# Attention stages: the low parts of the weights move to GpSimd, and the softmax's bias addition and row maximum become one VectorE instruction

## The chip, the cores and the metric

The kernel runs on one core of a Trainium2 chip. The metric is the device time of one execution in microseconds (us). Engines are named as in the profile: PE is TensorE (PEld its weight loads), DVE is VectorE, ACT is ScalarE, POOL is GpSimd, SP is SyncE, which issues the DMAs.

## The reference

The kernel computes a decoder trunk of two layers on 512 tokens of width 1024, with 16 heads of 64. Both layers add attention, a SwiGLU feed-forward part and a gated per-layer embedding to the residual `h`. Layer 0 attends by stick-breaking, layer 1 by a softmax with forget gates:

```python
# layer 0, mixer A
z = einsum('bhqd,bhkd->bhqk', qb, k) * scale
log_one_minus = where(strict, -softplus(z), 0.0)
later = cumsum(log_one_minus, axis=3, reverse=True) - log_one_minus
w = where(strict, exp(log_sigmoid(z) + later), 0.0)
out = einsum('bhqk,bhkd->bhqd', w, v)
# layer 1, mixer B
logits = einsum('bhqd,bhkd->bhqk', qb, k) * scale + fb[..., :, None] - f_cum[:, :, None, :]
logits = where(causal, logits, -inf)
out = einsum('bhqk,bhkd->bhqd', softmax(logits, axis=-1), v)
# both layers, afterwards
h = h + out @ w_o
h = h + (silu(g) * u) @ w_d          # g, u from rms(h) @ w_gu
h = h + sigmoid(rms(h) @ w_gate) * (p[i] @ w_proj)
```

The term `fb[..., :, None]` is the same for a whole row of the logits, so a softmax over the row does not change when it is left out.

## The kernel before

Every dense product is made of three matmuls, because each operand is split into a rounded high part and a remainder: `wh·xh`, `wh·xl` and `wl·xh` (L246 to L248; L389 to L391 where tokens are the rows). The weights arrive in 216 units of 128x1024. For each unit `load_unit` issues the DMA into `raw`, multiplies `raw` by a gain on POOL for 24 units of layer 1 (L144), casts it to `wh` on ACT (L147), and subtracts, `wl = raw - wh`, on DVE through `minus` (L125). `raw`, `wh` and `wl` have three buffers each, and units are loaded two ahead of their use.

An attention stage goes over 16 heads. `front(hd)` makes the scores of a head in three tiles `z` in PSUM: 512 wide, 384 wide, and one of 256 and 128 together; so there are four segments to a head. In layer 0 ACT forms two sigmoids `e` and `w` of a tile, DVE runs a scan over `e` for each segment (L638) and multiplies `w` by it (L641). In layer 1 DVE adds to `z` a per-row number `ngt` and a per-column row `gb` (L645), takes the maximum of each row (L651) and negates it (L653); ACT makes the exponential with that as bias and with a row sum (L655), DVE the reciprocal, and ACT the scaling. `back(hd)` turns the weights of the head with PE transposes (`pt`, L692) in three groups of four, four and two blocks, splits each group into a high part on ACT (`w3h`, `w2h`, `w1h`, L693) and a remainder on DVE (`w3l`, `w2l`, `w1l`, through `minus`, L125), and multiplies both by the values into `po` (L700, L701). Between these steps a `Filler` emits matmuls of later projections, so that PE has work while a head's chain runs on DVE and ACT.

`forget()` stands before the heads of layer 1. It makes the cumulated gate `gex` with a scan (L481) and a subtraction (L482), writes it to DRAM (`gdram`), from where `front` reads a row per head into `gb`, and transposes it on PE into `ngt` (L490 to L492).

A framework scheduler decides in which order instructions stand in each engine's queue; each engine runs its queue in that order. The score tiles have two PSUM buffers in layer 0 and one in layer 1 (`ZB = (2, 1)`): in layer 1 PE can begin a tile only when DVE has read the one before. `LOW` says per layer which engine forms `wl` while an attention stage's `state["low"]` holds; the other stages use DVE.

Of the kernel before, what the change touches and what calls it, by code (L numbers as in the profile page):

```python
# [18 lines left out]
F32 = mybir.dt.float32  # L19
F32R = mybir.dt.float32r  # L20
AF = mybir.ActivationFunctionType
ALU = mybir.AluOpType
PSUM = bass.MemoryType.PSUM

P = 128
S = 512
# [14 lines left out]
C_KG, C_QG, C_BF = 56, 57, 58  # L41
# [44 lines left out]
def trunk(ctx, tc, xT, pT, small, wf, wall, out, dump=None):  # L86
    nc = tc.nc
# [9 lines left out]
    sm = const.tile([P, NG], F32, name="sm")  # L97
# [4 lines left out]
    ident = const.tile([P, P], F32, name="ident")  # L102
    make_identity(nc, ident)

    identb = const.tile([P, P], BF16, name="identb")
    nc.vector.tensor_copy(identb, ident)
    masks = []
    for i, op in enumerate((ALU.is_gt, ALU.is_ge)):
        mf = tp.tile([P, S], F32, name="mf", tag="ta")
        nc.gpsimd.memset(mf[:, :P], 0.0)  # L110
        nc.gpsimd.affine_select(out=mf[:, :P], in_=mf[:, :P], pattern=[[1, P]], compare_op=op,
                                fill=-1.0e30, base=0, channel_multiplier=-1)
        mb = const.tile([P, P], BF16, name=f"mask{i}")
        nc.vector.tensor_copy(mb, mf[:, :P])
        masks.append(mb)
    one = const.tile([P, 1], F32, name="one")
    nc.vector.memset(one, 1.0)
    gq8 = const.tile([P, 1], F32, name="gq8")
    nc.vector.tensor_scalar_mul(gq8, sm[:, C_QG:C_QG + 1], 0.125)

    def table(name):
        tc.keep_in_program_order(nc.scalar.preload_act_table_set(name))
# [14 lines left out]
    def load_unit(u):  # L137
        if u not in raws:
            fetch(u)
        raw = raws.pop(u)  # L140
        if u in gains:
            c0, nk = gains[u]
            r3 = raw.rearrange("p (k n) -> p k n", k=nk)
            nc.gpsimd.tensor_tensor(  # L144
                r3, r3, sm[:, c0:c0 + nk].unsqueeze(2).to_broadcast([P, nk, 1024 // nk]), ALU.mult)
        wh = wpool.tile([P, 1024], F32R, name=f"wh{u}", tag="wh")
        nc.scalar.copy(wh, raw)  # L147
        wl = wpool.tile([P, 1024], F32R, name=f"wl{u}", tag="wl")
        if state["low"] == "gpsimd":
            for c in range(0, 1024, 256):  # L150
                nc.gpsimd.tensor_tensor(wl[:, c:c + 256], raw[:, c:c + 256],
                                        wh[:, c:c + 256].bitcast(F32), ALU.subtract)
        else:
            minus(wl, raw, wh)
        units[u] = (wh, wl)
# [200 lines left out]
    def attention(layer, buf):  # L356
# [3 lines left out]
        with tc.tile_pool(name=f"pa{layer}", bufs=1, space=PSUM, reuse_waits="tile") as pa, \  # L360
# [62 lines left out]
            if stick:  # L423
# [4 lines left out]
                m, r = norm_sums(pz, "z")  # L428
# [30 lines left out]
            def forget():  # L459
# [19 lines left out]
                nc.vector.scalar_tensor_tensor(zf[:16], zf[:16], 0.0, ef[:16], ALU.min, ALU.subtract)  # L479
                gex = tp.tile([P, S], F32, name="gex", tag="ta")[:16]  # L480
                nc.vector.tensor_tensor_scan(gex, zf[:16], zf[:16], 0.0, ALU.add, ALU.bypass)  # L481
                nc.vector.tensor_tensor(gex, gex, zf[:16], ALU.subtract)  # L482
                if "gex" in dump:
                    nc.sync.dma_start(dump["gex"], gex)
                gdram = dpool.tile([16, S], F32, name="gdram")
                nc.sync.dma_start(gdram, gex)
                ngt = a1.tile([P, 4, 16], F32, name="ngt")
                gps = pz.tile([P, S], F32, name="gps", tag="n", bufs=1)
                for j in range(4):
                    nc.tensor.transpose(gps[:, j * 16:(j + 1) * 16], gex[:, j * P:(j + 1) * P],  # L490
                                        ident[:16, :16])
                nc.vector.tensor_scalar_mul(ngt, gps[:, :64].rearrange("p (j n) -> p j n", j=4), -1.0)  # L492
                return gdram, ngt

            dd = {}

# [119 lines left out]
            def front(hd):  # L616
# [6 lines left out]
                for ti, segs in enumerate(TILES):  # L623
# [5 lines left out]
                    z = z[:, :n]  # L629
# [11 lines left out]
                            nc.vector.tensor_tensor(w[:, c + 1:c + m], w[:, c + 1:c + m],  # L641
                                                    e[:, c:c + m - 1], ALU.mult)
                    else:
                        for j, c, m in segs:
                            nc.vector.scalar_tensor_tensor(  # L645
                                w[:, c:c + m], z[:, c:c + m], ngt[:, j, hd:hd + 1], gb[:, j * P:],
                                ALU.add, ALU.add)
                        mx = a2.tile([P, 4], F32, name="mx", tag="mx", bufs=4)
                        ns = len(segs)
                        for si, (j, c, m) in enumerate(segs):  # L650
                            nc.vector.tensor_reduce(mx[:, si:si + 1], w[:, c:c + m],  # L651
                                                    mybir.AxisListType.X, ALU.max)
                        nc.vector.tensor_scalar_mul(mx[:, :ns], mx[:, :ns], -1.0)  # L653
                        for si, (j, c, m) in enumerate(segs):
                            nc.scalar.activation(w[:, c:c + m], w[:, c:c + m], AF.Exp,  # L655
                                                 bias=mx[:, si:si + 1], accum_out=mx[:, 2 + si:3 + si])
                        nc.vector.reciprocal(mx[:, 2:2 + ns], mx[:, 2:2 + ns])
                        for si, (j, c, m) in enumerate(segs):
# [66 lines left out]
            if stick:  # L725
                run(raw_qk(0))
            else:
                def sums():
                    m, tok["r"] = norm_sums()

                    tok["em"] = a1.tile([P, 4], F32, name="em")
                    nc.vector.tensor_scalar_mul(tok["em"], m, EPS)

                run(group(0, sums))
                rb = norm_bounce(tok["r"])
                run(expand(0))
                gdram, ngt = forget()
            for e in attn_order(layer)[3 if stick else 2:]:
                i = int(e[1:])
                fill.add(e, (raw_qk(i) if i < RAW_PAIRS else qk(i)) if e[0] == "p" else expand(i) if e[0] == "e" else  # L740
# [59 lines left out]


AHEAD = 2
LOW = ("vector", "vector")
ZB = (2, 1)
TB = (2, 2)
WB = (6, 5)
# [117 lines left out]
```

## Time and profile before

| what | value |
|---|---|
| timed runs | 1405.8, 1407.05, 1407.12 us, median 1407.05 |
| the profiled execution's own time | 1405.01 us |
| its span | 1403.2 us |
| PE busy, share of the span | 1363.8 us, 97% |
| DVE busy | 848.7 us, 60% |
| ACT busy | 607.9 us, 43% |
| POOL busy | 50.2 us, 4% |

The span is the time from the first to the last instruction of the profiled execution; its own time has 1.8 us more around it. A busy share is an average over the whole span. Layer 0 attends from the start to about 270 us, layer 1 from about 690 to 970 us; what lies between and after is feed-forward and embedding, which the change leaves alone.

### The profile page before, as it was taken

What the parts mean: (1) busy time and instruction counts of PE and PEld (TensorE: products, weight loads), DVE (VectorE), ACT (ScalarE), POOL (GpSimd) and SP (SyncE); (2) the same over time, 40 slices, a digit from 0 to 9 for tenths busy, and PEclk for the clock granted to TensorE, in tenths of its full rate; (3) what the DMA queues carried; (4) which work ended last, traced back from release to release, by engine and by line L of the source; (5) the groups of instructions that cost most, each with busy time, mean ns of one, the idle gap of its engine ahead of it and who ended that gap; (6) DMA issues with size and microseconds to landing.
All of it is one profiled execution on the core that took longest, in us unless ns stands there. A gap on an engine that the chain in (4) does not pass through costs nothing.

```text
span 1403.2 us, 18111 instructions
## 1 busy us (share of the span) xinstructions
PE 1363.8 (97%) x7112; PEld 1150.5 (82%) x7112; DVE 848.7 (60%) x1379; ACT 607.9 (43%) x1014; POOL 50.2 (4%) x39
## 2 busy tenths in 40 slices
PE   7899999999999999999999999999999999999998
PEld 7678777788888888888788888987888888888887
DVE  6798878845444443333878888887454444433335
ACT  5565564633323232322446677776332323322312
POOL 0000000000000000000222212000000000000000
PEclk9999999999999999999999999999999999999999
DMA  5332232224333333332333333332233333333332
GB/s 181 98 82 77 75 87 67 82 88 120 91 105 91 101 95 99 96 96 77 90 115 92 96 94 94 97 104 74 72 118 105 90 105 90 95 101 96 99 83 90
DMA packets 45030, 133.71 MB, mean 95 GB/s; under 512 B 7936, under 2 KB 8320, under 8 KB 44944
## 3 DMA queue, kind: packets, MB, share of 16 engines
q1 hardware_dynamic: 44944, 132.54, 32.2%
q8 instruction: 56, 0.92, 0.3%
q14 instruction: 30, 0.25, 0.1%
HBM read 121.99 MB, written 2.14 MB: 88 GB/s over the span
## 4 chain that ended last, share of the span: by engine, by line
PE 78%; DVE 13%; ACT 4%; DMA 2%; issue 2%; SPq 0%; DVEq 0%; ACTq 0%
PE ps L246 21%; PE ps L247 21%; PE ps L248 21%; PE psv L390 2%; PE psv L391 2%; PE psv L389 2%; DVE e L638 2%; DVE wl L125 2%; PE po L701 2%; PE pt L692 1%; DMA row<-r 1%; PE po L700 1%; PE z L607 1%; DVE w L641 1%; ACT wh L147 1%
## 5 line engine op out<-in xcount | busy, mean ns | idle before, releaser
L246 PE MATMUL ps<-bh,wh 128*128 128x512 f32 (+1 forms) x1232 | 482.3, 393 | 3.3 <-ACT bh L720 2.0
L248 PE MATMUL ps<-bh,wl 128*128 128x512 f32 (+1 forms) x1232 | 478.4, 389 | 0.0
L247 PE MATMUL ps<-bl,wh 128*128 128x512 f32 (+1 forms) x1232 | 478.1, 388 | 0.0
L147 ACT CAST wh<-raw 128x1024 fp32r<-128x1024 f32 x216 | 226.6, 1050 | 489.8 <-PE ps L247 415.7
L125 DVE TENSOR_TENSOR wl<-raw,wh 128x1024 fp32r<-128x1024 f32 x216 | 263.9, 1222 | 173.7 <-ACT wh L147 173.4
L246 PEld LDWEIGHTS ps<-bh,wh 128*128 128x128 f32 x1232 | 232.3, 189 | 47.0 <-ACT bh L720 2.7
L248 PEld LDWEIGHTS ps<-bh,wl 128*128 128x128 f32 x1232 | 232.2, 188 | 46.6
L247 PEld LDWEIGHTS ps<-bl,wh 128*128 128x128 f32 x1232 | 232.3, 189 | 43.7 <-DVE bl L125 0.4
L389 PE MATMUL psv<-wh,bh 128*128 128x256 f32 x512 | 152.8, 299 | 10.9 <-ACT wh L147 8.9
L390 PE MATMUL psv<-wl,bh 128*128 128x256 f32 x512 | 147.9, 289 | 1.4 <-DVE wl L125 1.4
L391 PE MATMUL psv<-wh,bl 128*128 128x256 f32 x512 | 148.1, 289 | 0.1
L389 PEld LDWEIGHTS psv<-wh,bh 128*128 128x128 f32 x512 | 100.2, 196 | 11.8 <-ACT wh L147 9.1
L289 DVE TENSOR_TENSOR s<-s,ps 128x512 f32<-128x512 f32 x44 | 30.3, 688 | 128.1 <-PE ps L248 127.9
L390 PEld LDWEIGHTS psv<-wl,bh 128*128 128x128 f32 x512 | 100.3, 196 | 2.6 <-DVE wl L125 1.9
L391 PEld LDWEIGHTS psv<-wh,bl 128*128 128x128 f32 x512 | 100.1, 196 | 0.3 <-DVE bl L125 0.3
L287 DVE TENSOR_TENSOR s<-ps,rb 128x512 f32<-128x512 f32 x44 | 30.2, 691 | 97.2 <-PE ps L248 79.9
L246 PE MATMUL ps<-eh,wh 128*128 128x512 f32 x224 | 87.1, 389 | 0.0
L247 PE MATMUL ps<-el,wh 128*128 128x512 f32 x224 | 87.1, 389 | 0.0
L248 PE MATMUL ps<-eh,wl 128*128 128x512 f32 x224 | 87.1, 389 | 0.0
L144 POOL TENSOR_TENSOR raw<-raw,sm 128x1024 f32<-128x1024 f32 x24 | 47.7, 1989 | 183.1 <-DMA raw<-in_w_dram 117.0
L692 PE MATMUL pt<-ident,w 128*128 128x128 f32 x320 | 51.7, 274 | 0.3 <-DVE w L641 0.2
L638 DVE TENSOR_TENSOR_SCAN e<-e 128x512 f32<-128x512 f32 (+1 forms) x64 | 49.9, 812 | 1.0 <-ACT e L635 0.9
(149 smaller groups left out, 1538.9 us busy)
## 6 DMA issues: line engine op xcount, KB each, us to landing
raw<-in_w_dram SPq DMA_DIRECT2D x216, 512.0 KB, 3.6
kd<-ke SPq DMA_DIRECT2D x32, 128.0 KB, 2.2
ke<-kd SPq DMA_DIRECT2D x32, 128.0 KB, 2.2
gb<-gdram SPq DMA_DIRECT2D x16, 256.0 KB, 3.2
h<-in_x_dram SPq DMA_DIRECT2D x8, 256.0 KB, 5.7
out_dram<-h SPq DMA_DIRECT2D x7, 256.0 KB, 2.0
rb<-row SPq DMA_DIRECT2D x5, 256.0 KB, 5.1
pf<-in_p_dram SPq DMA_DIRECT2D x2, 512.0 KB, 4.2
```

The costliest lines, as they stand in the source:

```text
L125: nc.vector.tensor_tensor(out, a, b.bitcast(F32), ALU.subtract)
L144: nc.gpsimd.tensor_tensor(r3, r3, sm[:, c0:c0 + nk].unsqueeze(2).to_broadcast([P, nk, 1024 // nk]), ALU.mult)
L147: nc.scalar.copy(wh, raw)
L246: nc.tensor.matmul(ps, wh, xh, start=first, stop=False)
L247: nc.tensor.matmul(ps, wh, xl, start=False, stop=False)
L248: nc.tensor.matmul(ps, wl, xh, start=False, stop=last)
L289: nc.vector.tensor_tensor(s, s, u, ALU.mult)
L389: nc.tensor.matmul(ps[:, st], xh, wh, start=first, stop=False)
L390: nc.tensor.matmul(ps[:, st], xh, wl, start=False, stop=False)
L391: nc.tensor.matmul(ps[:, st], xl, wh, start=False, stop=lastk)
L638: nc.vector.tensor_tensor_scan(e[:, c:c + m], e[:, c:c + m], e[:, c:c + m], 1.0, ALU.mult, ALU.bypass)
L692: nc.tensor.transpose(pt[:, bi * P:(bi + 1) * P], blk(j, s), ident)
```

## The change

- `LOW` becomes `("gpsimd", "gpsimd")`: in the attention stages `wl` is formed on POOL, one instruction for a unit. 24 units of layer 0 and 28 of layer 1 move.
- In layer 1 addition and row maximum become one instruction per segment, `tensor_tensor_reduce`. It works on negated scores (the query gain is -0.125 and the mask fills with +1e30), adds `gb` and takes the row minimum, which is then the bias of an exponential with scale -1. The program has two DVE rows for it, the operation and a 128x1 read of its accumulator. The separate reduce and the negation go.
- `ngt` is left out, with its four PE transposes and the DVE copy, and the subtraction of `gex` changes its sign.

```diff
-    for i, op in enumerate((ALU.is_gt, ALU.is_ge)):
+    for i, (op, fill) in enumerate(((ALU.is_gt, -1.0e30), (ALU.is_ge, 1.0e30))):
...
-    nc.vector.tensor_scalar_mul(gq8, sm[:, C_QG:C_QG + 1], 0.125)
+    nc.vector.tensor_scalar_mul(gq8, sm[:, C_QG:C_QG + 1], -0.125)
...
         if state["low"] == "gpsimd":
-            for c in range(0, 1024, 256):
-                nc.gpsimd.tensor_tensor(wl[:, c:c + 256], raw[:, c:c + 256],
-                                        wh[:, c:c + 256].bitcast(F32), ALU.subtract)
+            nc.gpsimd.tensor_tensor(wl, raw, wh.bitcast(F32), ALU.subtract)
...
-                nc.vector.tensor_tensor(gex, gex, zf[:16], ALU.subtract)
+                nc.vector.tensor_tensor(gex, zf[:16], gex, ALU.subtract)
...
-                ngt = a1.tile([P, 4, 16], F32, name="ngt")
-                gps = pz.tile([P, S], F32, name="gps", tag="n", bufs=1)
-                for j in range(4):
-                    nc.tensor.transpose(gps[:, j * 16:(j + 1) * 16], gex[:, j * P:(j + 1) * P],
-                                        ident[:16, :16])
-                nc.vector.tensor_scalar_mul(ngt, gps[:, :64].rearrange("p (j n) -> p j n", j=4), -1.0)
-                return gdram, ngt
+                return gdram
...
-                        for j, c, m in segs:
-                            nc.vector.scalar_tensor_tensor(
-                                w[:, c:c + m], z[:, c:c + m], ngt[:, j, hd:hd + 1], gb[:, j * P:],
-                                ALU.add, ALU.add)
                         mx = a2.tile([P, 4], F32, name="mx", tag="mx", bufs=4)
                         ns = len(segs)
                         for si, (j, c, m) in enumerate(segs):
-                            nc.vector.tensor_reduce(mx[:, si:si + 1], w[:, c:c + m],
-                                                    mybir.AxisListType.X, ALU.max)
-                        nc.vector.tensor_scalar_mul(mx[:, :ns], mx[:, :ns], -1.0)
+                            nc.vector.tensor_tensor_reduce(
+                                w[:, c:c + m], z[:, c:c + m], gb[:, j * P:], 1.0, 3.0e38,
+                                ALU.add, ALU.min, mx[:, si:si + 1])
                         for si, (j, c, m) in enumerate(segs):
-                            nc.scalar.activation(w[:, c:c + m], w[:, c:c + m], AF.Exp,
+                            nc.scalar.activation(w[:, c:c + m], w[:, c:c + m], AF.Exp, scale=-1.0,
                                                  bias=mx[:, si:si + 1], accum_out=mx[:, 2 + si:3 + si])
...
-LOW = ("vector", "vector")
+LOW = ("gpsimd", "gpsimd")
```

The lines of the changed program are some nine lower than before: the scan of layer 0 is L631, its product L634, `minus` L126, the subtraction on POOL L151, the gain L145, and the scores L600 to L603.

The first place is DVE's queue in layer 0, in a middle head, from the end of one head's product to the remainder of the next head's first group. The scan appears there as a SCALAR_TENSOR_TENSOR of L638. Before:

```order
L718 TENSOR_TENSOR at<-at,po 64x512
L125 TENSOR_TENSOR v<-psv,v 128x8x64
L125 TENSOR_TENSOR wl_1313<-raw_1309,wh_1311 128x1024
L638 SCALAR_TENSOR_TENSOR e<-e 128x512
L638 SCALAR_TENSOR_TENSOR e<-e 128x384
L641 TENSOR_TENSOR w<-w,e 128x511
L641 TENSOR_TENSOR w<-w,e 128x383
L638 SCALAR_TENSOR_TENSOR e<-e 128x256
L638 SCALAR_TENSOR_TENSOR e<-e 128x128
L641 TENSOR_TENSOR w<-w,e 128x255
L641 TENSOR_TENSOR w<-w,e 128x127
L125 TENSOR_TENSOR w3l<-pt,w3h 128x512
```

The same place of the changed program:

```order
L709 TENSOR_TENSOR at<-at,po 64x512
L126 TENSOR_TENSOR v<-psv,v 128x8x64
L631 SCALAR_TENSOR_TENSOR e<-e 128x512
L634 TENSOR_TENSOR w<-w,e 128x511
L631 SCALAR_TENSOR_TENSOR e<-e 128x384
L631 SCALAR_TENSOR_TENSOR e<-e 128x256
L634 TENSOR_TENSOR w<-w,e 128x383
L634 TENSOR_TENSOR w<-w,e 128x255
L631 SCALAR_TENSOR_TENSOR e<-e 128x128
L634 TENSOR_TENSOR w<-w,e 128x127
L126 TENSOR_TENSOR w3l<-pt,w3h 128x512
```

The subtraction that stood between `v` and the first scan is gone from DVE, and scans and products alternate in another order; nothing else of the eleven rows has moved. The other queues of this stage change from head 5 on only in that POOL gets the subtraction; in heads 0 to 4 the scheduler has also moved the casts of ACT.

The second place is POOL's queue at the start of layer 1's attention. Before, gains alone stand there, one after the other:

```order
L144 TENSOR_TENSOR raw_5518<-raw_5518,sm 128x1024
L144 TENSOR_TENSOR raw_5549<-raw_5549,sm 128x1024
L144 TENSOR_TENSOR raw_5679<-raw_5679,sm 128x1024
L144 TENSOR_TENSOR raw_5710<-raw_5710,sm 128x1024
L144 TENSOR_TENSOR raw_5934<-raw_5934,sm 128x1024
L144 TENSOR_TENSOR raw_5965<-raw_5965,sm 128x1024
```

In the changed program:

```order
L145 TENSOR_TENSOR raw_5518<-raw_5518,sm 128x1024
L145 TENSOR_TENSOR raw_5549<-raw_5549,sm 128x1024
L151 TENSOR_TENSOR wl_5523<-raw_5518,wh_5521 128x1024
L145 TENSOR_TENSOR raw_5679<-raw_5679,sm 128x1024
L145 TENSOR_TENSOR raw_5710<-raw_5710,sm 128x1024
L151 TENSOR_TENSOR wl_5554<-raw_5549,wh_5552 128x1024
L151 TENSOR_TENSOR wl_5684<-raw_5679,wh_5682 128x1024
L145 TENSOR_TENSOR raw_5920<-raw_5920,sm 128x1024
L145 TENSOR_TENSOR raw_5951<-raw_5951,sm 128x1024
L151 TENSOR_TENSOR wl_5715<-raw_5710,wh_5713 128x1024
```

Subtractions and gains now share the queue, and the subtraction of a unit can stand behind the gain of the unit one or two later, which waits for that unit's DMA.

The third place is PE's queue in head 6 of layer 1, between the 512-wide score tile and the 384-wide one, which share the one PSUM buffer; `psv` are the filler's matmuls. Before, these rows end a run of 14 filler matmuls (three more stand above them):

```order
L389 MATMUL psv<-wh_6847,bh_105 128x256
L390 MATMUL psv<-wl_6849,bh_105 128x256
L391 MATMUL psv<-wh_6847,bl_107 128x256
L389 MATMUL psv<-wh_6847,bh_105 128x256
L390 MATMUL psv<-wl_6849,bh_105 128x256
L391 MATMUL psv<-wh_6847,bl_107 128x256
L389 MATMUL psv<-wh_6847,bh_105 128x256
L390 MATMUL psv<-wl_6849,bh_105 128x256
L391 MATMUL psv<-wh_6847,bl_107 128x256
L389 MATMUL psv<-wh_6847,bh_105 128x256
L390 MATMUL psv<-wl_6849,bh_105 128x256
L607 MATMUL z<-ke,qd 128x384
```

In the changed program the whole run, behind the last matmul of the 512-wide tile:

```order
L603 MATMUL z<-mask_98,identb 128x128
L388 MATMUL psv<-wh_6805,bh_105 128x256
L389 MATMUL psv<-wl_6807,bh_105 128x256
L390 MATMUL psv<-wh_6805,bl_107 128x256
L388 MATMUL psv<-wh_6805,bh_105 128x256
L389 MATMUL psv<-wl_6807,bh_105 128x256
L390 MATMUL psv<-wh_6805,bl_107 128x256
L388 MATMUL psv<-wh_6805,bh_105 128x256
L389 MATMUL psv<-wl_6807,bh_105 128x256
L600 MATMUL z<-ke,qd 128x384
```

The scheduler has taken six of the 14 filler matmuls out of this place. Over the 16 heads the run is exactly eight long ten times, before twice; in head 0, beside `forget`, it has 66 matmuls (62 of the filler and four transposes `qt`) where it had 53 (45 of the filler, four `gps` and four `qt`).

## Rows read from the trace of the kernel before

**Rows 1.** The page: busy time of each engine, share of the span, instructions.

```profile
PE 1363.8 (97%) x7112; PEld 1150.5 (82%) x7112; DVE 848.7 (60%) x1379; ACT 607.9 (43%) x1014; POOL 50.2 (4%) x39
```

**Rows 2.** Windows: length, busy PE, PEld, DVE, ACT, POOL, then granted clock.

```profile
40.00:100.00 60.00, 53.97 (x259) 41.93 (x258) 52.30 (x81) 36.76 (x65) 0.00 (x0) 0.97 0.29 78
100.00:265.00 165.00, 159.00 (x915) 129.91 (x914) 135.34 (x211) 94.14 (x174) 0.00 (x0) 1.00 0.29 80
690.00:745.00 55.00, 47.61 (x344) 43.91 (x343) 42.62 (x77) 22.51 (x42) 15.92 (x8) 0.94 0.32 94
745.00:955.00 210.00, 205.65 (x1503) 185.93 (x1502) 185.51 (x429) 155.82 (x350) 27.24 (x14) 1.00 0.35 99
713.50:716.90 3.40, 3.40 (x19) 3.40 (x18) 3.40 (x13) 0.16 (x2) 1.25 (x1) 0.50 0.63 210
```

**Rows 3.** The page's groups: the gain on POOL.

```profile
L144 POOL TENSOR_TENSOR raw<-raw,sm 128x1024 f32<-128x1024 f32 x24 | 47.7, 1989 | 183.1 <-DMA raw<-in_w_dram 117.0
```

**Rows 4.** Groups by form, DVE in layer 0: busy us, mean ns, idle before.

```profile
L125 DVE TENSOR_TENSOR wl<-raw,wh 128x1024 fp32r<-128x1024 f32 x31 | 37.9, 1222 | 17.3 <-ACT wh L147 17.3
L638 DVE TENSOR_TENSOR_SCAN e<-e 128x512 f32<-128x512 f32 x16 | 19.5, 1220 | 1.0 <-ACT e L635 0.9
```

**Rows 5.** Timeline of POOL and DVE at 736 us: start, length.

```profile
736.05 2.11 POOL L144 TENSOR_TENSOR raw<-raw,sm 128x1024 f32<-128x1024 f32 x1 [0.19 <-DMA raw<-in_w_dram]
736.44 2.80 DVE L481 TENSOR_TENSOR_SCAN gex<-zf 16x512 f32<-16x512 f32 x1
```

**Rows 6.** Waits of PE, 100 to 265 us: total, times, longest.

```profile
PE po L701 <- DVE w3l L125: 5.9, 12, 1.0
```

**Rows 7.** Timeline of a head of layer 0 around 127 us.

```profile
127.02 0.60 ACT L635 ACTIVATE e<-z 128x512 f32<-128x512 f32 x1
127.16 1.23 DVE L125 TENSOR_TENSOR wl<-raw,wh 128x1024 fp32r<-128x1024 f32 x1 [0.25 <-ACT wh L147]
...
128.30 2.07 DVE L638 TENSOR_TENSOR_SCAN e<-e 128x512 f32<-128x512 f32 x2
...
133.50 0.51 PE L701 MATMUL po<-w3l,v 128*128 128x512 f32 x1 [0.19 <-DVE w3l L125]
```

**Rows 8.** Timeline: the subtraction of the last such head.

```profile
206.70 1.23 DVE L125 TENSOR_TENSOR wl<-raw,wh 128x1024 fp32r<-128x1024 f32 x1 [0.28 <-ACT wh L147]
```

**Rows 9.** Timeline of another head of layer 0, 223 to 228 us.

```profile
223.55 1.05 ACT L147 CAST wh<-raw 128x1024 fp32r<-128x1024 f32 x1 [0.34 <-PE ps L247]
...
226.79 0.69 DVE L125 TENSOR_TENSOR w3l<-pt,w3h 128x512 fp32r<-128x512 f32 x1
...
227.39 1.22 DVE L125 TENSOR_TENSOR wl<-raw,wh 128x1024 fp32r<-128x1024 f32 x1
...
227.53 0.49 PE L701 MATMUL po<-w3l,v 128*128 128x512 f32 x1 [0.59 <-DVE w3l L125]
```

**Rows 10.** Timeline at the start of layer 1's attention.

```profile
710.61 1.23 DVE L125 TENSOR_TENSOR wl<-raw,wh 128x1024 fp32r<-128x1024 f32 x1 [0.25 <-ACT wh L147]
...
711.96 0.38 PE L389 MATMUL psv<-wh,bh 128*128 128x256 f32 x1 [1.32 <-DVE m L223]
...
740.09 0.39 PE L490 MATMUL gps<-ident,gex 16*128 16x16 f32 x4 [2.37 <-DVE gex L482]
...
746.76 0.74 DVE L645 SCALAR_TENSOR_TENSOR w<-z,ngt,gb 128x512 f32<-128x512 f32 x1
```

**Rows 11.** Groups by form, DVE in layer 1's softmax (columns as in Rows 4).

```profile
L645 DVE SCALAR_TENSOR_TENSOR w<-z,ngt,gb 128x512 f32<-128x512 f32 x16 | 11.9, 746 | 0.4 <-PE z L610 0.2
L651 DVE TENSOR_REDUCE mx<-w 128x1 f32<-128x512 f32 x16 | 10.8, 678 | 0.1
L653 DVE TENSOR_SCALAR mx<-mx 128x2 f32<-128x2 f32 x16 | 5.0, 312 | 0.1
```

**Rows 12.** Groups, ACT from 745 to 955 us: reads of its accumulator.

```profile
L655 ACT ACTIVATION_READ_ACCUMULATOR w<-w,mx 128x1 f32 x61 | 11.5, 189 | 0.0
```

**Rows 13.** Timeline: PE at the end of layer 1's attention.

```profile
965.23 0.96 PE L246 MATMUL ps<-bh,wh 128*128 128x512 f32 x3 [2.04 <-ACT bh L720]
```

More of the change, by code (lines that the diff above doesn't have):

```diff
@@ L111, in trunk @@
         nc.gpsimd.affine_select(out=mf[:, :P], in_=mf[:, :P], pattern=[[1, P]], compare_op=op,
-                                fill=-1.0e30, base=0, channel_multiplier=-1)
+                                fill=fill, base=0, channel_multiplier=-1)
         mb = const.tile([P, P], BF16, name=f"mask{i}")
@@ L736, in attention @@
                 run(expand(0))
-                gdram, ngt = forget()
+                gdram = forget()
             for e in attn_order(layer)[3 if stick else 2:]:
```

## The prediction

> **What bounds the kernel now.** I read the page first: PE is busy 97% of the span, DVE 60%, POOL 4% [rows 1]. So time on DVE or POOL counts only where PE waits for it. Then I read the attention stages by windows [rows 2]. Idle time of PE is the length minus the busy time: 60.00 - 53.97 = 6.0 us in the early heads of layer 0, 165.00 - 159.00 = 6.0 us in the later ones, 55.00 - 47.61 = 7.4 us at the start of layer 1 and 210.00 - 205.65 = 4.4 us in its middle. DVE is busy for 185.51 of those 210 us, and yet PE hardly waits: the filler matmuls cover DVE. So although the change takes much work off DVE, at most these few microseconds can come back, and any chain that the filler doesn't cover can lose. In the later heads of layer 0 nearly the whole idle time is one wait, PE for `w3l`: 5.9 us in 12 of the heads [rows 6]. There a head's chain (scores, scans, products, transposes, `w3h`, `w3l`) is as long as its cover, so what delays a scan delays PE.
>
> **Part 1, the subtraction on POOL, layer 0.** DVE loses 24 instructions of 1.222 us [rows 4], 29 us, where PE waits for other things. On POOL I take the price of the gain, which has the same shape: 47.7/24 = 1.99 us on average [rows 3]; 1.9 where DVE does not disturb it. PE needs a unit many microseconds after it is formed, so the longer subtraction itself costs nothing: no wait of PE for `wl` stands in the later heads' 6.0 us beside the 5.9 for `w3l`.
>
> What it can cost shows where POOL and DVE overlap. At 736 us a gain on POOL starts 0.39 us before a scan on DVE, and this scan, 512 elements wide, lasts 2.80 us [rows 5], where one of that width takes 1.220 [rows 4]: 1.58 us lost. POOL was to end at 736.05 + 2.11 = 738.16, and 736.44 + 2.80 - 1.22 = 738.02: the scan really began when POOL let go, 0.14 before its recorded end. So a DVE instruction with both inputs in SBUF waits for the whole POOL instruction. The Trainium skill's page "SBUF — State Buffer", section "Who interferes with whom", states this: DVE's second read interface is the one GpSimd has, and whoever comes first keeps it for a whole instruction. By that rule, the trace agrees (2.80 against 1.220 us). The scans and products of layer 0 have both inputs in SBUF; `w3l` and its kin read PSUM.
>
> Now head by head. In the head around 127 us the cast ends when `wl` can start, at 127.16; `wl` takes DVE until the scan begins at 128.30, though its `e` was there at 127.02 + 0.60 = 127.62 [rows 7]. After the change POOL holds from about 127.13 to 127.13 + 1.95 - 0.14 = 128.95, with 1.95 between its two prices. The scan begins 0.65 us later than before. PE already waits for `w3l` in this head (0.19 at 133.50), so the delay goes to PE. Four heads, up to the one at 206.7 [rows 8], have this place: **+2.6**. One more, near 234 us, where scan and cast come a little apart: **+0.4**. In two heads (near 144 and 198 us) the cast ends among the scans: DVE saves nothing on their path and POOL cuts in between two of them, but `wl` stood before `w3l` and leaves it; net I take **+0.5** each. In two heads `wl` stood behind `w3l`, as at 227.39 after 226.79, although the cast had ended at 223.55 + 1.05 = 224.60 [rows 9], among scans and products. There nothing is saved and POOL holds them in full: 1.75 us each, **+3.5**. Other heads have PSUM readers behind the cast: 0. With -0.2 for a `w3l` that loses a `wl` ahead of it, the later heads come to 2.6 + 0.4 + 1.0 + 3.5 - 0.2 = **+7.3**. If POOL does not cut in between queued instructions of DVE, the last two kinds fall to about 0 and the sum to +3.
>
> The two long stalls would then be 0.59 + 1.75 = 2.3 us, and a stall can cost more than itself: after the one of 1.32 us at 711.96 [rows 10] the granted clock stood at 0.50, the lower of its two levels, for 3.40 us [rows 2], in which half the work, 1.7 us, is lost. I count one such drop: **+1.7** (0 to 3.4). Early heads: DVE is busy 52.30 of 60 us [rows 2] and loses some eight `wl`, 9.8 us; but the scheduler moved casts and POOL cuts in here too. Between -3 and +3, I take **-1**. Layer 0 together: 7.3 + 1.7 - 1 = **+8**.
>
> A price for POOL from a page alone: "GPSIMD Engine Reference", section 3.1, in the Trainium skill measures elementwise work with two inputs on GpSimd 1.96 times as long as on VectorE, an estimate of 2.4 us here; the eight held heads would then cost some 0.4 more each, +3 in all. The nearest row (1.9 to 1.99) decides, and the sum goes by it.
>
> **Part 2, layer 1.** DVE loses 28 x 1.22 = 34 us here too. The fused instruction has the inputs of the addition (PSUM and SBUF), so its bounds are 746 ns, the addition of 512 [rows 11], and 1220 ns, the scan of 512 [rows 4], the slowest row of that width. I take 746, since it too streams two inputs once, plus a read of the accumulator, at most ACT's 189 ns [rows 12]. The reduce of 678 ns and the negation of 312 [rows 11] go. All this is DVE time that the filler hid; it moves PE only at these places:
> - At 711.96 PE waits 1.32 us for `m`, which stands behind a `wl` of 1.23 us on DVE [rows 10]. On POOL that `wl` is out of its way, and `m` reads PSUM: **-1.2**.
> - Beside `forget`, PE waits 2.37 us for `gex` before the transposes into `ngt` [rows 10]. They go, and a small wait for the first keys with them (0.4). Late next is the row `gb`, which comes over DRAM: the first addition runs at 746.76, and the 384-wide tile needs its buffer. The 66 covering matmuls at some 0.12 us reach about 745.6, so a wait of about 1.3 appears: **-1.4**, between -2.5 and +1.
> - Without these stalls two clock drops of 1.7 may go; I take one: **-1.7**.
> - At the end of the stage PE waits 2.04 for the last head [rows 13]; its chain loses reduce and negation, 0.68 + 0.31: **-1.0**.
> - In the middle some 2 of the 4.4 us idle come back. Against it stands the single score buffer: ten heads now have eight matmuls, 8 x 0.12 = 0.96 us, between two tiles that share it, where the fused instruction takes 0.75 + up to 0.19 and waits its turn on DVE for some 0.3. That is 0.3 short, ten times: +3. I take **0**; with 1.22 us for the fused instruction it is +8 - 2 = +6.
>
> POOL's queue: a subtraction can stand behind the gain of a later unit, but 52 instructions of 1.9 us are 99 us of some 280, and PE has several microseconds before it wants a unit: 0.
>
> Layer 1 together: -1.2 - 1.4 - 1.7 - 1.0 + 0 = **-5.3**, between -10 and +4.
>
> **Sum.** The profiled execution took 1405.01 us; +8 - 5.3 gives 1407.7. The median of the runs shown is 2.0 above it, so on its scale I predict **1410**, 0.2% slower. About 0.2%, 2.8 us, is also what a measurement of this kernel can tell from no change.
>
> **Rivals.**
> 1. *Layer 1's gains are larger than layer 0's loss.* If POOL does not cut in among queued DVE instructions (layer 0: +3 - 1 and no clock drop = +2) and layer 1 gives 7, the time is 1407.05 - 5 = 1402. It decides from the point where the held scans cost under 5 us. For it speaks that all overlaps seen have POOL first by a clear margin; against it that PE has no slack behind the scans. Chance 0.25.
> 2. *It cancels.* Held scans cost 5, layer 1 gives 5: 1407. Chance 0.28.
> 3. *The forecast:* holds win by some 3 us: 1410. Chance 0.32.
> 4. *The fused instruction is as slow as the scan, or the score buffer is late in most heads:* the middle of layer 1 costs +6 and not 0, or POOL's price is above 1.99 us: 1416 to 1420. Chance 0.15.
>
> Slower by over 0.2% is rival 4 and most of the forecast: 0.44; within 0.2% is rival 2 and the rest: 0.31; faster 0.25. The likeliest case alone spans 1407 to 1414; the range for 8 in 10 reaches to the others: 1400 to 1420.
>
> **What would show it.** The `w3l` wait of PE from 100 to 265 us grows from 5.9 to about 13; scans there last up to 3 us when POOL overlaps; the wait for `m` is gone and one for `gb` stands near 746; fused instructions of 512 take near 0.75 us; PE waits for DVE before the 384-wide tiles, some 0.3 each. I am wrong if scans keep their 1.22 us beside POOL, if the early heads gain or lose more than 3 us, or if the scheduler's smaller cover in layer 1 costs PE over half a microsecond per head.

## The result and the profile after

The changed kernel takes 1446.34 us (median of 4 runs, 1443.23 to 1446.47), the kernel before 1406.42 us (4 runs): ratio 1.0279, 95% interval 1.0262 to 1.0297. The prediction was 1410, between 1400 and 1420. The profiled execution has a span of 1441.4 us, 38.2 us more than before. One run of the experiment kgqc below, 1518.72 us at a granted clock of 0.85, belongs to a slower state of the chip and is left out of its median.

I compared both traces at marks on PE: the last `po` of layer 0, the first score tile of layer 1 and its last `po`. From the start to layer 0's last `po` the changed kernel is 21.5 us longer; from there to layer 1's first score tile 11.5 us, of which 9.6 lie between `forget` and that tile; over the heads of layer 1 6.6 us; behind them 1.4 us shorter. Layer 0, with a forecast of +8, loses 21.5 us, and what follows it, with a forecast of -5.3, loses 16.7.

The page of the changed kernel, busy times, answers to [rows 1]:

```profile
PE 1373.1 (95%) x7108; PEld 1156.6 (80%) x7108; DVE 803.6 (56%) x1278; ACT 609.3 (42%) x1014; POOL 174.7 (12%) x91
```

DVE is 45 us less busy, POOL 124 us more: the work moved as meant, and the time grew. Windows of the changed kernel (columns as in [rows 2]) show PE's side of it:

```profile
100.00:285.00 185.00, 166.76 (x934) 135.19 (x933) 133.55 (x197) 95.49 (x176) 43.48 (x18) 0.98 0.26 71
715.00:770.00 55.00, 39.30 (x277) 35.70 (x276) 35.89 (x66) 19.97 (x37) 25.34 (x12) 0.86 0.27 78
761.50:775.10 13.60, 5.31 (x23) 4.82 (x24) 3.45 (x5) 2.50 (x5) 3.72 (x2) 0.50 0.33 80
```

PE idles 18.2 us in the later heads of layer 0, where it idled 6.0; at the start of layer 1 it idles 15.7 instead of 7.4, and for 13.6 us around the longest stall the granted clock is at the lower of its two levels. The prices, by groups and forms, of POOL's subtraction, of layer 0's 512-wide scan, and of the fused instruction with its read (in a profile it has the name CUSTOM_DVE_ANT_0):

```profile
L151 POOL TENSOR_TENSOR wl<-raw,wh 128x1024 fp32r<-128x1024 f32 x52 | 126.0, 2423 | 303.1 <-ACT wh L148 298.3 <-PE po L692 2.5 <-PE ps L247 2.3
L631 DVE TENSOR_TENSOR_SCAN e<-e 128x512 f32<-128x512 f32 x16 | 29.4, 1839 | 7.9 <-ACT e L628 7.9
L642 DVE CUSTOM_DVE_ANT_0 w<-z,gb 128x512 f32<-128x512 f32 x16 | 11.0, 688 | 5.1 <-PE z L603 5.0
L642 DVE DVE_READ_ACCUMULATOR2_ANT mx<- 128x1 f32 x64 | 5.3, 83 | 0.0
```

The fused instruction is cheap: 0.688 + 0.083 us where the addition and the reduce took 0.746 + 0.678 [rows 11]. The subtraction on POOL takes 2.42 us, not 1.95. And the 512-wide scans of layer 0 last 1.84 us on average where they lasted 1.22 [rows 4].

Layer 0, one head in the timeline of the changed kernel, the place of [rows 7] (here and in the later timelines only the rows that the text reads are shown):

```profile
132.93 0.60 ACT L628 ACTIVATE e<-z 128x512 f32<-128x512 f32 x1
133.11 2.40 POOL L151 TENSOR_TENSOR wl<-raw,wh 128x1024 fp32r<-128x1024 f32 x1 [1.94 <-ACT wh L148]
133.56 3.03 DVE L631 TENSOR_TENSOR_SCAN e<-e 128x512 f32<-128x512 f32 x1 [0.75 <-ACT e L628]
...
137.07 0.69 DVE L634 TENSOR_TENSOR w<-w,e 128x511 f32<-128x511 f32 x1 [0.48 <-ACT w3h L684]
...
140.57 0.68 DVE L126 TENSOR_TENSOR w3l<-pt,w3h 128x512 fp32r<-128x512 f32 x1
...
141.31 0.49 PE L692 MATMUL po<-w3l,v 128*128 128x512 f32 x1 [2.09 <-DVE w3l L126]
```

The scan is ready at 133.56 and lasts 3.03 us: 1.22 of work behind 1.8 of waiting for POOL. PE's wait for `w3l` at the end of the head is 2.09 us where it was 0.19. Over the stage this wait grew from 5.9 us [rows 6] to 17.7 us (waits of PE, 100 to 285 us):

```profile
PE po L692 <- DVE w3l L126: 17.7, 13, 2.8
```

Layer 1's long stall, in the timeline of the changed kernel (SPq is SyncE's queue; two DMAs of `raw` stand in one row, and it took 10.87 us until both were issued):

```profile
752.39 0.33 SPq L240 DMA_DIRECT2D rb<-row  x1
752.81 10.87 SPq L136 DMA_DIRECT2D raw<-in_w_dram  x2
...
758.21 1.52 DVE L506 SCALAR_TENSOR_TENSOR kd<-qt,sm,ke 64x512 fp32r<-64x512 f32 x2
758.95 1.89 POOL L145 TENSOR_TENSOR raw<-raw,sm 128x1024 f32<-128x1024 f32 x1 [9.64 <-DMA raw<-in_w_dram]
760.80 2.52 POOL L151 TENSOR_TENSOR wl<-raw,wh 128x1024 fp32r<-128x1024 f32 x1
763.74 1.11 SPq L516 DMA_DIRECT2D kd<-ke  x2
764.89 1.25 SPq L516 DMA_DIRECT2D ke<-kd  x2
...
769.79 0.77 PE L600 MATMUL z<-ke,qd 128*128 128x512 f32 x1 [10.66 <-DMA ke<-kd]
```

Read it from the end. PE waits 10.66 us for the key copies. These are issued at 763.74, although `kd` was formed by 759.73, because they stand in SP's queue behind the second `raw` DMA. That DMA waits for its buffer, which comes free when the subtraction of an earlier unit ends, at 763.32. The subtraction stood in POOL's queue behind the gain of a later unit, and POOL waited 9.64 us for that unit's DMA, the first of the two, issued at 752.81. It is the order of POOL's queue shown above, and its price is paid three queues on. That first DMA stands in SP's queue directly behind the small read `rb<-row`, so part of POOL's wait is a weight DMA held by a small transfer; the runs below do not touch this place, and in kgq POOL still waits 9.66 us there.

### The profile page after: what moved, and what is told of

It reads as the page before. It is cut to its first block, busy times and chain, and to the rows that moved or that the text cites. A ratio compares the mean times of both kernels' runs of the same rounds, so it can differ in the third digit from the quotient of the medians.

```text
span 1441.4 us, 18087 instructions
## 1 busy us (share of the span) xinstructions
PE 1373.1 (95%) x7108; PEld 1156.6 (80%) x7108; DVE 803.6 (56%) x1278; ACT 609.3 (42%) x1014; POOL 174.7 (12%) x91
## 4 chain that ended last, share of the span: by engine, by line
PE 69%; DVE 7%; ACT 4%; DMA 3%; issue 1%; POOL 0%; DVEq 0%; ACTq 0%
PE ps L245 20%; PE ps L247 20%; PE ps L246 20%; PE psv L388 2%; PE psv L390 2%; PE psv L389 2%; DMA row<-r 1%; PE pt L683 1%; PE po L692 1%; PE z L600 1%; DMA rb<-row 1%; PE po L691 1%; DVE wl L126 1%; DVE e L631 1%; DVE h L266 1%
## 5 line engine op out<-in xcount | busy, mean ns | idle before, releaser
L126 DVE TENSOR_TENSOR wl<-raw,wh 128x1024 fp32r<-128x1024 f32 x164 | 200.6, 1223 | 154.4 <-ACT wh L148 153.9
L151 POOL TENSOR_TENSOR wl<-raw,wh 128x1024 fp32r<-128x1024 f32 x52 | 126.0, 2423 | 303.1 <-ACT wh L148 298.3
L631 DVE TENSOR_TENSOR_SCAN e<-e 128x512 f32<-128x512 f32 (+1 forms) x64 | 60.2, 967 | 8.8 <-ACT e L628 8.6
L600 PE MATMUL z<-ke,qd 128*128 128x256 f32 (+2 forms) x128 | 47.2, 369 | 15.9 <-DMA ke<-kd 12.2
```

The source lines that it names most:

```text
L126: nc.vector.tensor_tensor(out, a, b.bitcast(F32), ALU.subtract)
L151: nc.gpsimd.tensor_tensor(wl, raw, wh.bitcast(F32), ALU.subtract)
L600: nc.tensor.matmul(zt[:, c:c + n], qd[:, t], ke[:, s0:s0 + n], start=True, stop=False)
L631: nc.vector.tensor_tensor_scan(e[:, c:c + m], e[:, c:c + m], e[:, c:c + m], 1.0, ALU.mult, ALU.bypass)
```

## The experiments

Theory A: POOL's subtraction holds DVE instructions with two SBUF inputs, and in layer 0 those on the chain. Theory B: in layer 1 waits at the head of in-order queues carry a late buffer over to small transfers. The rival of both was the scheduler's other order. In the runs sub0 to sub0c the base is the kernel before.

**sub0 and sub1: each layer's subtraction alone, in the kernel before.**

```diff
-            for c in range(0, 1024, 256):
-                nc.gpsimd.tensor_tensor(wl[:, c:c + 256], raw[:, c:c + 256],
-                                        wh[:, c:c + 256].bitcast(F32), ALU.subtract)
+            nc.gpsimd.tensor_tensor(wl, raw, wh.bitcast(F32), ALU.subtract)
...
-LOW = ("vector", "vector")
+LOW = ("gpsimd", "vector")      # sub1: ("vector", "gpsimd")
```

> The kernel before, with layer 0's subtractions alone on GpSimd (one instruction per unit). Theory A, the subtraction holds DVE's scans and products: nearly all of layer 0's loss of the change returns, +18 to +23 us (1424 to 1430), 512-wide scans average near 1.8 us and PE waits near 2 us for w3l in about eight heads. Rival, the loss comes from the scheduler's other order of layer 0 and not from the hold: scans keep 1.2 us and the loss stays under 8 us.

> The kernel before, with layer 1's subtractions alone on GpSimd. Theory B, a subtraction queued behind a later unit's gain frees a raw buffer late, the DMA for it blocks SP's queue and the key DMAs behind it: PE waits over 5 us for the first score tile and the time is +8 to +20 us. Rival, layer 1's loss belongs to the fused instruction and the order it brings: no long wait, within 3 us of before.

sub0: 1426.5 us, ratio 1.0148 (1.0131 to 1.0165); `w3l` waits 17.7 us, 512-wide scans 1840 ns: at layer 0's last `po` it is 20.5 us behind the kernel before, nearly all of the change's 21.5, as theory A says. sub1: 1427.44 us, 1.0147 (1.0132 to 1.0162), a little over what was expected, with a wait of 9.2 us before the first score tile (waits of PE in sub1, 690 to 1005 us), without the fused instruction:

```profile
PE z L605 <- DMA ke<-kd: 9.2, 1, 9.2
PE po L699 <- DVE w2l L125: 4.7, 4, 2.1
PE qt L595 <- DVE qd L511: 2.9, 2, 2.1
```

**fused: the fused instruction alone,** the changed kernel with `LOW = ("vector", "vector")`.

> The changed kernel with all subtractions on VectorE, so the fused addition and row minimum alone. If the fused instruction is as cheap as the addition and its read (0.75 + 0.1 us) it gives 2 to 7 us, 1399 to 1404. Rival, the smaller cover before the 384-wide tiles costs PE more than the removed instructions give: 0 to +6 us.

1398.79 us, ratio 0.9948 (0.9933 to 0.9963). This part gives some 7 us, at the edge of what was expected, and beats both kernels. In its middle stretch DVE is busy for 157.74 of 210 us where it was 185.51 [rows 2], and PE 204.66 where it was 205.65: as forecast, the time doesn't come from there. The score buffer costs little: PE waits 2.8 us in three places, not in ten small ones, and 2.29 us of it stand before the first 384-wide tile, where the fused instruction itself waits for the row `gb` (waits of PE in fused, 690 to 970 us):

```profile
PE z L600 <- DVE mx L642: 2.8, 3, 2.3
```

The three parts multiply to 1.0148 x 1.0147 x 0.9948 = 1.024, a little under the 1.0279 of the whole.

**sub0p and sub0s: which subtractions cost.** Each moves some of layer 0's units by what DVE does next in the kernel before.

```diff
-        if state["low"] == "gpsimd":
+        if state["low"] == "gpsimd" and u in (15, 17, 20, 21, 23, 26, 29):          # sub0p
+        if state["low"] == "gpsimd" and u in (16, 18, 19, 22, 24, 25, 27, 28, 30):  # sub0s
```

> The kernel before, with seven of layer 0's subtractions on GpSimd: those whose cast ends where VectorE's next instructions read PSUM (units 15, 17, 20, 21, 23, 26, 29). Theory A, only the hold of scans and products costs: within 2.5 us of before (1404 to 1409). Rival, a subtraction on GpSimd costs wherever it stands (units come later, buffers come free later): 7/24 of the loss of all, +5 to +7 us.

> The kernel before, with eight of layer 0's subtractions on GpSimd: those whose cast ends where scans or products come next (units 16, 18, 19, 22, 24, 25, 27, 28). Theory A: nearly the whole loss of the later heads, +11 to +17 us (1417 to 1424), about 1.9 us each. Rival: 8/24 of the loss of all, +6 to +8 us.

sub0p: 1407.59 us, ratio 1.0008 (0.9998 to 1.0017). sub0s: 1419.27 us, 1.0102 (1.0081 to 1.0122); it moved eight units, since unit 30 is loaded after the stage and stays on DVE. In sub0p no scan or product overlaps a subtraction. Seven moves beside PSUM readers cost nothing that can be told, eight beside scans 13 to 14 us, 1.7 each. The rival, a price wherever the subtraction stands, falls. The nine other units of the stage were moved by neither run. The scan in sub0p and in sub0s, by forms:

```profile
L636 DVE TENSOR_TENSOR_SCAN e<-e 128x512 f32<-128x512 f32 x16 | 19.5, 1220 | 1.2 <-ACT e L633 1.1
```

```profile
L636 DVE TENSOR_TENSOR_SCAN e<-e 128x512 f32<-128x512 f32 x16 | 28.2, 1764 | 4.7 <-ACT e L633 4.6
```

**sub0z: the scan with one SBUF input.** sub0 with the scan's unused second operand taken from PSUM.

```diff
-tensor_tensor_scan(e[:, c:c + m], e[:, c:c + m], e[:, c:c + m], 1.0,
+tensor_tensor_scan(e[:, c:c + m], e[:, c:c + m], z[:, c:c + m], 1.0,
```

> Layer 0's subtractions on GpSimd, and the scan's second operand, which its operation doesn't use, is the score tile in PSUM and not the tile in SBUF. Theory A, the hold hits an instruction with both inputs in SBUF: 512-wide scans beside a subtraction keep 1.2 to 1.3 us and PE's w3l waits fall, though the products may still be held and the score tiles are freed later; 1408 to 1421 us. Rival, any VectorE instruction is held or the scan for another reason: the average 512-wide scan stays at 1.8 us and the time at 1424 us or more.

1417.78 us, ratio 1.0075 (1.0059 to 1.0091), 9 us back. All 24 subtractions are still on POOL, and the scan is back at its old length, by forms and in one head of the timeline (two scans, 512 and 384 wide, in one row):

```profile
L636 DVE TENSOR_TENSOR_SCAN e<-e,z 128x512 f32<-128x512 f32 x16 | 19.5, 1218 | 11.0 <-ACT w L634 10.1 <-PE z L608 0.8
```

```profile
137.23 2.40 POOL L150 TENSOR_TENSOR wl<-raw,wh 128x1024 fp32r<-128x1024 f32 x1 [1.97 <-ACT wh L147]
138.17 2.06 DVE L636 TENSOR_TENSOR_SCAN e<-e,z 128x512 f32<-128x512 f32 x2 [1.24 <-ACT w L634]
```

The scan begins 0.94 us after the subtraction, well inside it, and isn't held; four more of the 16 heads show the same. So the hold asks for two SBUF inputs. PE's waits in sub0z, 100 to 285 us, show what is left:

```profile
PE po L699 <- DVE w3l L125: 4.9, 4, 2.4
PE z L605 <- DVE e L636: 4.1, 12, 0.4
```

The products still read two SBUF tiles, and the score tile is now freed only by the scan, 4.1 us in 12 heads. By the heads' last `po`, heads 5 to 15 lose 2.9 us where they lose 15.4 in sub0; but heads 0 to 4 lose 10.0 where they lose 5.1 in sub0, and no run shows why. "SBUF — State Buffer" in the Trainium skill, section "Who interferes with whom", says that a DVE instruction with at most one SBUF input, outside the two-port modes, does not contend with GpSimd; the trace agrees (1218 ns against 1840).

**sub0c: shorter holds.** The kernel before with `LOW = ("gpsimd", "vector")` and its old code: four pieces of 256 columns.

> Layer 0's subtractions on GpSimd in four pieces of 256 columns each. Theory A with the hold lasting one GpSimd instruction: a scan waits for one piece, some 0.6 us, and not for 2.4; 1410 to 1419 us. Rival, each piece gets in between two VectorE instructions, so that the sum of the holds stays: 1423 to 1430 us.

1415.83 us, ratio 1.007 (1.0055 to 1.0085): half of the loss. Timeline of sub0c:

```profile
130.04 4.20 POOL L151 TENSOR_TENSOR wl<-raw,wh 128x256 fp32r<-128x256 f32 x4 [1.51 <-ACT wh L147]
130.49 1.37 DVE L638 TENSOR_TENSOR_SCAN e<-e 128x512 f32<-128x512 f32 x1 [0.75 <-ACT e L635]
132.35 1.28 DVE L641 TENSOR_TENSOR w<-w,e 128x511 f32<-128x511 f32 x1 [0.49 <-DVE e L638]
```

The scan loses 0.15 us instead of 1.8, the next product some 0.6 (1.28 us, where the changed kernel shows 0.69), and POOL's four pieces now take 4.2 us between them, where four pieces of the usual length take some 3.0 (0.74 us is the median of the 96 pieces, 0.91 the mean): each side waits for the other in turn.

**kq and kgq: the queue of layer 1's small DMAs,** the changed kernel with the key copies (kq), and the reads of `gb` too (kgq), issued by ScalarE.

```diff
-                            nc.sync.dma_start(a[i][other[i]].bitcast(F32), b[i][mine[i]].bitcast(F32))
+                            (nc.sync if stick else nc.scalar).dma_start(a[i][other[i]].bitcast(F32), b[i][mine[i]].bitcast(F32))
...
-                    nc.sync.dma_start(gb, gdram[hd:hd + 1, :].to_broadcast([P, S]))
+                    nc.scalar.dma_start(gb, gdram[hd:hd + 1, :].to_broadcast([P, S]))    # kgq
```

> The changed kernel with layer 1's key copies (the DMAs between the two key tiles) issued by ScalarE and not by SyncE. Theory B, they stand in SP's queue behind a weight DMA that waits for its buffer: PE's wait of 10.7 us before the first score tile falls to 2 to 4 us, and with less time at the low clock the kernel gains 8 to 13 us (1433 to 1438). Rival, the keys themselves are late because the normalization row comes over DRAM: the wait falls by under 3 us and the time by under 4.

> The run kq with the reads of the gate row issued by ScalarE as well, so that no small DMA of layer 1's heads stands behind a weight DMA in SyncE's queue. Theory B: the wait of 4.8 us for the second score tile, which kq shows for that row, falls under 2 us; with kq's effect kept the time is 1430 to 1438 us. Against it: a read that waits blocks ScalarE's own casts, which can take the gain away (1438 to 1446 us). Rival, the row is late by itself: the wait stays over 4 us.

kq: 1442.18 us, ratio 1.0248 (1.0225 to 1.027). The wait before the first score tile fell from 10.66 to 3.17 us, within the expectation; the time did not follow, because the second tile now waits. Timeline of kq:

```profile
767.75 4.75 POOL L151 TENSOR_TENSOR wl<-raw,wh 128x1024 fp32r<-128x1024 f32 x2
770.18 0.34 SPq L136 DMA_DIRECT2D raw<-in_w_dram  x1
770.63 1.05 SPq L615 DMA_DIRECT2D gb<-gdram  x2
...
775.92 0.69 DVE L642 CUSTOM_DVE_ANT_0 w<-z,gb 128x512 f32<-128x512 f32 x1 [4.60 <-DMA gb<-gdram]
...
776.77 0.66 PE L600 MATMUL z<-ke,qd 128*128 128x384 f32 x1 [4.82 <-DVE mx L642]
```

The read of `gb` is issued directly behind a weight DMA that waited for the subtractions, the same block one transfer later. kgq takes both out of the queue: 1433.24 us, 1.0185 (1.0168 to 1.0203), 13 us under the changed kernel, with 1.22 us before the first tile and 0.81 before the second. The queue is shown as a cause.

**sub1g and sub1gc: gains off GpSimd, then shorter holds.** sub1 with the gain of L144 on VectorE, and the same with the four pieces.

```diff
-            nc.gpsimd.tensor_tensor(
+            nc.vector.tensor_tensor(
                 r3, r3, sm[:, c0:c0 + nk].unsqueeze(2).to_broadcast([P, nk, 1024 // nk]), ALU.mult)
```

> Layer 1's subtractions on GpSimd as in the run sub1, and the gains of layer 1 on VectorE, so that no subtraction stands behind a gain that waits for a DMA. Theory B: buffers come free when the cast is done, PE's wait before the first score tile falls from 9.2 us to under 3, and the time from 1427 to 1411 to 1420 us; what is left is VectorE held by the subtractions. Rival, the wait comes from the schedule or from the keys themselves: it stays over 6 us and the time above 1423 us.

> As sub1g, with each subtraction in four pieces of 256 columns. If the rest of layer 1's loss is VectorE held for a whole subtraction, short instructions on the queries' norms above all, the pieces give 3 to 8 us against sub1g. Rival, the rest is of the schedule's making: within 2 us of sub1g.

sub1g: 1426.46 us, ratio 1.0139 (1.0122 to 1.0155): the rival's time, but not its wait. The wait before the score tile is gone, but one of 6.71 us for `qn` is there a little earlier. Timeline of sub1g:

```profile
727.59 2.38 POOL L150 TENSOR_TENSOR wl<-raw,wh 128x1024 fp32r<-128x1024 f32 x1 [1.50 <-ACT wh L147]
727.91 2.08 DVE L572 TENSOR_TENSOR u<-r 128x8 f32<-128x8 f32 x1
727.92 2.40 SPq L135 DMA_DIRECT2D raw<-in_w_dram  x2
...
734.87 1.23 DVE L144 TENSOR_TENSOR raw<-raw,sm 128x1024 f32<-128x1024 f32 x1 [4.88 <-DMA raw<-in_w_dram]
736.01 0.16 DVE L573 SCALAR_TENSOR_TENSOR u<-u,mm 128x8 f32<-128x8 f32 x1
```

On DVE the gain waits for the weights' DMA, and behind it wait three of the four short instructions of a norm that ends in `qn`. The wait at a queue's head has only moved to another queue. A second thing stands there: `u<-r`, 8 columns wide, lasts 2.08 us beside POOL.

sub1gc: 1421.03 us, 1.0099 (1.0081 to 1.0117), 5 us under sub1g: the holds are a part of layer 1's loss too. In the traces the gain is in the heads, 7.7 us shorter than in sub1g. In the changed kernel `u<-r` takes 804 ns on average, in the kernel before 266 (groups by form of DVE, changed kernel and before):

```profile
L567 DVE TENSOR_TENSOR u<-r 128x8 f32<-128x8 f32 x16 | 12.9, 804 | 4.9 <-ACT r L566 4.8
```

```profile
L574 DVE TENSOR_TENSOR u<-r 128x8 f32<-128x8 f32 x16 | 4.2, 266 | 1.3 <-ACT r L573 1.1
```

**kgqc: both causes relieved in the whole change,** kgq with the four pieces.

> The run kgq with every subtraction in four pieces of 256 columns: both mechanisms relieved in the whole change. If they are the causes and add up, kgq's 1433 us falls by some 10 for layer 0 (as sub0c against sub0) and some 5 for layer 1 (as sub1gc against sub1g), to 1415 to 1422 us. Rival, the pieces fill GpSimd's queue and delay units in layer 1: it stays above 1426 us.

1418.28 us, ratio 1.0097 (1.0078 to 1.0116): about two thirds of the change's loss are back while all 52 subtractions stay on POOL. By the marks its trace is 10.5 us behind the kernel before at layer 0's last `po`, and only 2.7 us more by the end: of layer 1's 16.7 us most is gone.

**fusedg, fusedh, fusedk, fusedhk: is there more in it without subtractions on GpSimd?** fused with all gains on VectorE; with those from layer 1's ninth unit on; with kgq's DMAs on ScalarE; and the last two together.

> The fused instruction alone, as in the run fused, with the gains of layer 1 on VectorE too, so that GpSimd does nothing beside it. If the holds by gains still cost something in layer 1 (the gate's scan ahead of the first row), it is 1 to 3 us faster than fused: 1395 to 1398. Rival, 24 more instructions on VectorE cost as much as the holds: within 1.5 us of fused, or slower.

> The fused instruction alone, with the gains of the first eight units of layer 1 on GpSimd and the other 16 on VectorE. In the run fusedg the stretch of the heads was 9 us shorter than in fused and the start 4.5 us longer, with a wait of 2.9 us where a gain stands in VectorE's queue. If the two are separate, the start is as in fused and the heads keep some of the gain: 1394 to 1398 us. Rival, the shorter stretch of the heads only means that more filler ran ahead of them: within 1.5 us of fused, 1397 to 1400 us.

> The fused instruction alone, with the key copies and the reads of the gate row in layer 1 issued by ScalarE. If SyncE's queue still holds small transfers behind weight DMAs there (fused has PE waits of 1.9 us for a key copy and 2.3 us for the gate row), it gives 1 to 4 us, 1395 to 1398 us. Rival, these waits belong to the transfers and their sources themselves, or ScalarE loses as much: within 1.5 us of fused or slower.

> fusedh and fusedk together. If both give something by separate waits: 1392 to 1396 us. Rival: no better than the better of the two within 1.5 us.

Ratios to the kernel before: fusedg 0.9951 (0.9936 to 0.9966), fusedh 0.9972 (0.9962 to 0.9982), fusedk 0.9956 (0.9942 to 0.997), fusedhk 0.9946 (0.9934 to 0.9959). None is faster than fused's 0.9948 by what the intervals can tell, and fusedh is rather slower: the shorter stretch of heads in fusedg's trace did not become time. The rivals held, and fused, the smallest edit, stays the version to take.

## Why the prediction was wrong

The bound was read rightly: time off DVE that the filler hides gave nothing, and PE's waits decided. The mechanism of layer 0 was named and is shown (sub0s, sub0p, sub0z), and the fused instruction's price was about right (0.69 + 0.08 us). That its part gave 7 us, beside a forecast of -5.3 for all of layer 1, is in part luck. The -1.2 for `m` belonged to the subtractions; of the -1.4 at `forget` next to nothing came (2.29 us of waiting for `gb` in place of 2.37 for `gex`); and the stage's end gave 0.46 and not 1.0. One stretch at the lower clock did go, the one behind the stage's end (0.50 from 966.10 to 969.50 in the kernel before, 1.00 at that place of fused, 963.50 to 967.00), and not one at the two stalls that I had named. The trace of fused, its slowest run, is 3.6 us shorter than before, 1.8 in layer 1's heads and 1.4 behind them; where the rest of the 7 us comes from is not shown.

Four terms were wrong.

- **The hold's size in layer 0: +7.3 for the later heads, measured some 12, and +1.7 for the clock, measured some 3.3** (sub0's heads 5 to 15 together slip from 5.1 to 20.5 us behind before). PE's wait for `w3l` grew by 17.7 - 5.9 = 11.8 us. Two stretches of the changed kernel's later heads are at the lower clock, where the kernel before has none [rows 2]; by the prediction's measure they lose half of PE's 3.40 and 3.25 us of work (windows of the changed kernel):

```profile
157.30:160.70 3.40, 3.40 (x12) 2.87 (x12) 0.72 (x2) 0.37 (x1) 0.00 (x0) 0.50 0.69 195
246.00:249.40 3.40, 3.25 (x9) 2.57 (x10) 1.64 (x4) 0.37 (x1) 0.00 (x0) 0.51 0.12 45
```

In the head shown the scan's work begins at 133.56 + 3.03 - 1.22 = 135.37, 1.84 us after its `e`; before it began 0.68 after it [rows 7]. That is 1.16 where I had 0.65. Nearly all of the missing half is POOL's price: I took the gain's row [rows 3], 1.95, and set an estimate of 2.4 aside; 2.40 was measured here and 2.42 on average. "GPSIMD Engine Reference" in the Trainium skill, section 3.1, has the ratio 1.96, and the trace agrees: 2.42 against 1.22. The gain's second input is a few broadcast columns, the subtraction's a whole tile; that this is why it is slower was not tried. From the scan's true start to `w3l` this head takes 5.20 us and took 4.46; 0.48 of it is idle time of DVE between the scan and the product that reads it and, in the new order, stands right behind it. That much is this head's alone: in the eight others with this order the product begins 0.10 us after its scan, and why it is 0.48 here stays open. 1.16 + 0.74 = 1.9 is what `w3l`'s wait grew by (0.19 to 2.09). In sub0s the four heads of this kind slip 1.5 to 1.6 us each, where I had 0.65. One of my nine heads, the one at 251 us, had no moved unit at all.

- **The early heads: -1, measured +5.9.** I had named a change of over 3 us here as a sign of being wrong. The last `po` of head 4 comes 5.9 us later than before, 5.1 in sub0; in sub0s, whose units stand behind these heads, it is 0.6 earlier. At least one hold of theory A is in it: a product of 383 columns, 0.54 us long in the kernel before, lasts 2.45 beside a subtraction, and PE waits 2.51 us behind it (timeline of the changed kernel). What makes up the rest stays open.

```profile
56.91 2.65 POOL L151 TENSOR_TENSOR wl<-raw,wh 128x1024 fp32r<-128x1024 f32 x1 [6.70 <-ACT wh L148]
57.53 2.45 DVE L634 TENSOR_TENSOR w<-w,e 128x383 f32<-128x383 f32 x1
...
60.03 0.44 PE L683 MATMUL pt<-ident,w 128*128 128x128 f32 x2 [2.51 <-DVE w L634]
```

- **"POOL's queue ... 0".** The units were indeed in time for PE. But the weight DMA behind a late buffer blocks SP's queue, and key copies and gate rows stand in it: 10.66 us before the first score tile, with 13.6 us at the lower clock level around it, in which PE was busy for 5.31 us, so some 2.7 us more. I asked who waits for the unit, and not who stands behind the DMA that waits for the unit's buffer.
- **"All this is DVE time that the filler hid".** True of the time removed, not of the holds added: short instructions of the norms with two SBUF inputs (`u<-r`) wait for whole subtractions, and `qt`, `qd` and the remainders wait behind them. sub1gc's 5 us and the waits of sub1 show a part of it. How layer 1's loss divides exactly between the queue, these holds and the scheduler's order stays open: sub1gc is still 14 us above before, and kgqc, which relieves the first two, leaves 2.7 us of its 16.7 in the trace.

Of the smaller terms, the wait for `m` fell from 1.32 to 0.25 us in the changed kernel, as forecast. The wait at the stage's end fell from 2.04 [rows 13] to 1.58, by 0.46 and not 1.0. The clock did not gain: the stalls that were removed had others in their place, and the mean granted clock of the profiled execution fell from 0.995 to 0.986.

## What to carry to other kernels

Work moved to an idle engine is free only if nothing on the busy path shares a port or a queue with it: before moving it, list which instructions of the other engine take two SBUF inputs while it runs, and follow the buffers that the moved work frees to the DMA that waits for them and to everything behind that DMA in its queue. Where a price is missing, take the row that reads the same operands, not only one of the same shape. And try the parts of a change apart: here one part gives 0.5% and two take 1.5% each.

## What was not expected of the hardware

An instruction of eight columns, 0.17 us alone, lasts 2.08 us beside a subtraction on POOL (sub1g): the hold lasts until the other engine's instruction ends, however short the own one is. Cutting that instruction into four keeps the hold short but stretches POOL's work from 2.4 to 4.2 us in the head shown, partly since four pieces need 3.0 us by themselves, partly since POOL then waits as well.

A product that stands directly behind the scan whose output it reads begins only 0.10 us after the scan's end, here after 222.10 + 2.90 = 225.00 (timeline of the changed kernel; so in eight of the nine such places):

```profile
222.10 2.90 DVE L631 TENSOR_TENSOR_SCAN e<-e 128x512 f32<-128x512 f32 x1 [0.93 <-ACT e L628]
225.10 0.69 DVE L634 TENSOR_TENSOR w<-w,e 128x511 f32<-128x511 f32 x1
```

So such an order costs little by itself; the 0.48 us of the head at 137.07 and the 0.49 of sub0c at 132.35 are the exception.
